# Three input transfers at the head of an encoder layer: the norm's row to GpSimd's queue, a token tile from ScalarE's queue to SyncE's

## The chip, the cores and the metric

The kernel runs on one core of one Trainium2 chip. A core has TensorE (matrix products), VectorE and ScalarE (elementwise work), GpSimd (called POOL in the profile) and SyncE (SP), which only issues transfers. SP, ScalarE and POOL each have a queue of their own for transfers; the core's 16 DMA engines carry out what the three queues hand them. The metric is the device time of one execution in microseconds (us), and the smaller is the better.

## The reference

One layer of an encoder over 1024 tokens of 1024 float32 values:

```python
h = swiglu(rmsnorm(x, ffn1_pre_g), w_gate, w_up, w_down)
x = x + 0.5 * rmsnorm(h, ffn1_post_g)
...                                  # neighbourhood and dilated attention
x = x + 0.5 * rmsnorm(swiglu(rmsnorm(x, ffn2_pre_g), ...), ffn2_post_g)

def rmsnorm(x, g):
    y = xf * lax.rsqrt(jnp.mean(xf * xf, axis=-1, keepdims=True) + NORM_EPS)
    return y * g
def swiglu(x, w_gate, w_up, w_down):
    return (jax.nn.silu(x @ w_gate) * (x @ w_up)) @ w_down
```

The change touches only the start of the first line: the norm of the first 512 tokens with the gain row `ffn1_pre_g`, and the first products with `w_gate`.

## The kernel before

A matrix product is done in three TensorE passes over operands that are split into a high and a low part of a rounded format (`hi`, `lo`: ScalarE rounds with a copy, VectorE subtracts). The products of a 2x2 block scheme follow one another for the whole program; the profile's lines L466, L467 and L472 are the three passes of the first feed-forward product, L783 the second.

Nothing of that can start before the first 512 tokens are normed and transposed. This is the head of the program, and it is written out by hand, in the order in which each engine is to run it (`ordered` keeps that order on TensorE, VectorE and ScalarE):

- `x0` is the input; `xs[0]` to `xs[3]` are tiles of 128 tokens. Tiles 0 and 1 are loaded in two halves of 512 columns each, tiles 2 and 3 whole. In the trace all are `x<-in_x_dram`: L1637 for the halves, L1648 for tile 2, L1649 for tile 3.
- The gain row (4 KB, one partition) goes to the first row of `xn[0]` (L1639, `xn<-in_ffn_pre_g_dram`). `spread_gain` has TensorE multiply it by a row of ones, so that PSUM holds it in all 128 partitions (L344, `gps`), in two halves of two passes each. ScalarE copies each half to `gain` (L345).
- `square` forms sums of squares: ScalarE for tile 0 and for the first half of tile 1 (L166), VectorE for the second half (L1665). `rstd_by_sqrt` makes 1/sqrt of them: two small steps on VectorE (L330, L331), a square root on ScalarE (L332), four more on VectorE.
- `scaled` multiplies the tokens by that and by the gain (L1672, VectorE), `op0.one` transposes them on TensorE (L174) and splits them (L181, L182).
- `graw` are the raw weights of the first blocks, in halves: L1647 the first halves of blocks 0 and 1, L1651 the second halves, L1652 block 2. `parts` splits them (`hi0`, `lo0`, ..., L1683 and L1686).

On ScalarE the order is: square of tile 0, square of tile 1's first half, first gain copy, square root, `hi0`, second gain copy, square of tile 2, the two splits of the transposed tiles, `hi1`, square of tile 3's half.

Each transfer signals one of eight semaphores, which the framework gives out in turn, apart for the hardware queues (SP and ScalarE) and for POOL's; the ninth transfer waits for the one that had its semaphore before.

Of the kernel before, what the change touches and what calls it, by code (L numbers as in the profile page):

```python
# [336 lines left out]
def spread_gain(c, t, row, one):  # L337

    nc = c.nc
    copies = []  # L340
    for h in range(2):
        sl = slice(h * T, h * T + T)
        ps = c.psm.tile([P, T], F32, tag="mm", name="gps")
        nc.tensor.matmul(ps, one, row[:, sl], start=True, stop=True)  # L344
        copies.append(lambda sl=sl, ps=ps: nc.scalar.copy(t[:, sl], ps))  # L345
    return t, *copies
# [1052 lines left out]
def layer(tc, a, out):  # L1399
    nc = tc.nc  # L1400
    c = Ctx(tc)
    with ExitStack() as ctx:
# [26 lines left out]
        x0 = [a["x"][t * P:(t + 1) * P, :] for t in range(8)]  # L1429
# [51 lines left out]
        def gate_pairs(which, op, wg, wu, early):  # L1481
            return PairGemm(c, op, [(wg[f], wu[f]) for f in range(NF)], early, GatePairs(c, which))

        def ffn(which, op, prep, pg, get, turns, sums, more, post, pre, src, dst, begin=None, tables=()):
# [7 lines left out]
            if begin:  # L1492
                left_pool(e)
            begun = begin(pg) if begin else ()
            plan(pg.early, turns)
            r = sub()
# [119 lines left out]
        with ExitStack() as order:  # L1616
# [9 lines left out]
            half = [slice(0, T), slice(T, D)]  # L1626
            first_junk = [c.xp.tile([P, D], F32, tag="s", name="junk", bufs=2)]
            w2 = c.xp.tile([P, D], F32, tag="x1", name="w2", bufs=2)
            xn = [c.xp.tile([P, D], F32, tag="xn", name="xn", bufs=c.xn) for _ in range(2)]
            gain = c.xp.tile([P, D], F32, tag="pre", name="gain", bufs=1)  # L1630
            xs = {t: c.xp.tile([P, D], F32, tag="x", name="x", bufs=4) for t in range(4)}
# [3 lines left out]
            for t in range(2):  # L1635
                for h, q in enumerate((nc.sync, nc.scalar)):
                    q.dma_start(xs[t][:, half[h]], x0[t][:, half[h]])  # L1637
                    if (t, h) == (0, 0):
                        nc.sync.dma_start(xn[0][:1], a["ffn1_pre_g"])  # L1639
            op0.gain, *gains = spread_gain(c, gain, xn[0][:1], xn[1][:1, :P])  # L1640

            def begin(pg):
                for b in range(2):
                    pg.raw[b] = c.wg.tile([P, 2, T], F32, tag="g", name="graw")
                pg.raw[2] = w2.rearrange("p (i x) -> p i x", i=2)
                for b in range(2):
                    nc.sync.dma_start(pg.raw[b][:, 0], pg.srcs[b][0][:, half[0]])  # L1647
                nc.scalar.dma_start(xs[2], x0[2])  # L1648
                nc.sync.dma_start(xs[3], x0[3])  # L1649
                for b in range(2):  # L1650
                    nc.sync.dma_start(pg.raw[b][:, 1], pg.srcs[b][0][:, half[1]])  # L1651
# [89 lines left out]
                while keeps:  # L1741
# [8 lines left out]
                                    {0: [F(4, 5), L(6, 7)], 2: [F(6, 7)], 3: [U(4)], 5: [U(5)], 6: [U(6)], 7: [U(7)]},  # L1750
                                    down_sums(a["wd1"], ts1), value_sums(a["wv"], tsv),
                                    a["ffn1_post_g"], a["mix_pre_g"], x0, x1, begin,
                                    bias_steps(c, *[a[k] for k in ("na_rel_bias", "t5_rel_bias", "onehot", "lncount", "cmask")]))

# [17 lines left out]
            pg = PairGemm(c, op, [(a["wqk"][p], a["wqk"][8 + p]) for p in QK_ORDER], 8, QKPairs(c))  # L1772
# [163 lines left out]
        with ordered():  # L1936
# [18 lines left out]
            pg = gate_pairs(3, op, a["wg2"], a["wu2"], 11)  # L1955
# [94 lines left out]
```

## Time and profile before

| | |
|---|---|
| time, median of 3 runs | 1828.1 us (1826.97 to 1828.38) |
| profiled execution, its own time | 1828.32 us |
| its span, first to last instruction | 1826.5 us |
| TensorE busy in the span | 1808.7 us, 99% |
| VectorE, ScalarE, POOL busy | 1309.8, 832.1, 352.3 us |

The span is 1.8 us shorter than the profiled execution's time, which is 0.2 us above the median of the runs. All times inside the program are counted from the start of the span. In a row of the timeline the first number is the start, the second how long the instruction (or the run of like instructions, with their count behind x) took; the bracket is how long the engine had been idle, and what ended it. "SPq" and "ACTq" are the issuing of transfers, not the transfers themselves.

### The profile page before, as it was taken

The page shows a single profiled execution, that of the slowest core. Times are in us where ns is not written, and L with a number is a line of the kernel's source. Part 1 is how long each engine was busy: PE and PEld are TensorE (multiplying, and loading weights), DVE is VectorE, ACT ScalarE, POOL GpSimd, SP SyncE. Part 2 cuts the span into 40 slices and gives each one's busy share as a digit, 9 for nine tenths or more (in the row PEclk, how much of TensorE's full clock was granted, in tenths as well). Part 3 has the DMA queues.
Part 4 walks back from the last instruction along what each step waited for, and adds up shares of the span by engine and source line. Part 5 has one row for each costly group of instructions (what it writes and reads, how often), then busy time and mean ns, then how long its engine had stood idle before and what let it go on. Part 6 is the DMA issues. An engine that isn't in the chain of part 4 may idle for free.

```text
span 1826.5 us, 25169 instructions
## 1 busy us (share of the span) xinstructions
PE 1808.7 (99%) x8876; PEld 1522.9 (83%) x8876; DVE 1309.8 (72%) x2225; ACT 832.1 (46%) x1495; POOL 352.3 (19%) x583
## 2 busy tenths in 40 slices
PE   8999999999999999999999999999999999999998
PEld 6888888888888888888999998888888888888886
DVE  6878877776466878477666856778877777664557
ACT  6622233334443656234688765654223333354433
POOL 2223321112021123232344100221111111110000
PEclk9999999999999999999999999999999999999999
DMA  7756566557888858868687523594655566596564
GB/s 277 263 182 215 166 226 224 203 208 260 306 302 307 288 200 265 265 226 294 198 264 254 184 97 116 192 309 162 196 179 196 201 221 223 185 349 196 193 230 143
DMA packets 172769, 409.28 MB, mean 224 GB/s; under 512 B 20401, under 2 KB 42321, under 8 KB 170594
## 3 DMA queue, kind: packets, MB, share of 16 engines
q1 hardware_dynamic: 124450, 246.07, 40.9%
q0 software_dynamic: 47184, 159.51, 24.0%
q10 hardware_dynamic: 1008, 2.10, 0.3%
q8 instruction: 70, 1.15, 0.3%
q14 instruction: 57, 0.47, 0.1%
HBM read 280.09 MB, written 132.56 MB: 226 GB/s over the span
## 4 chain that ended last, share of the span: by engine, by line
PE 92%; DVE 3%; DMA 2%; ACT 1%; issue 1%; SPq 0%; DVEq 0%; ACTq 0%
PE accp L783 26%; PE mmp L467 17%; PE mmp L466 17%; PE mmp L472 17%; PE po L1215 2%; PE ptp L1095 2%; PE po L1331 2%; PE accp L357 1%; PE accp L359 1%; PE accp L358 1%; PE sp L1182 1%; PE trp L174 1%; PE sp L1315 1%; DMA praw<-in_wd_dram 1%; DMA graw<-in_wg_dram 1%
## 5 line engine op out<-in xcount | busy, mean ns | idle before, releaser
L466 PE MATMUL mmp<-x,whi 128*128 128x512 f32 (+1 forms) x1464 | 571.8, 391 | 1.7 <-ACT x L181 1.4
L467 PE MATMUL mmp<-x,whi 128*128 128x512 f32 (+1 forms) x1464 | 569.2, 389 | 0.8 <-DVE x L182 0.7
L783 PE MATMUL accp<-pw 128*128 128x512 f32 x1800 | 411.2, 390 | 0.4 <-ACT hb L804 0.4
L783 PEld LDWEIGHTS accp<-pw 128*128 128x128 f32 x1800 | 337.2, 188 | 70.5 <-ACT hb L804 0.8
L472 PE MATMUL mmp<-x,wlo 128*128 128x512 f32 (+1 forms) x1464 | 390.6, 389 | 0.0
L466 PEld LDWEIGHTS mmp<-x,whi 128*128 128x128 f32 x1464 | 275.7, 188 | 59.6 <-ACT x L181 2.2
L467 PEld LDWEIGHTS mmp<-x,whi 128*128 128x128 f32 x1464 | 275.7, 188 | 57.4 <-DVE x L182 1.6
L472 PEld LDWEIGHTS mmp<-x,wlo 128*128 128x128 f32 x1464 | 274.7, 188 | 56.8
L751 DVE TENSOR_TENSOR pw<-praw,pw 128x1024 fp32r<-128x1024 f32 (+1 forms) x181 | 201.2, 1150 | 126.0 <-ACT pw L750 125.1
L750 ACT CAST pw<-praw 128x1024 fp32r<-128x1024 f32 (+1 forms) x181 | 168.8, 983 | 207.4 <-PE accp L783 162.6
L456 ACT CAST whi<-wraw 128x1024 fp32r<-128x1024 f32 x126 | 132.7, 1053 | 187.5 <-PE mmp L467 161.9
L457 DVE TENSOR_TENSOR wlo<-wraw,whi 128x1024 fp32r<-128x1024 f32 x126 | 153.3, 1218 | 2.5 <-ACT whi L456 2.5
L693 POOL DMA_DIRECT2D g<-sg x44 | 24.0, 545 | 428.5 <-DVE sg L686 243.0
L481 ACT COPY s<-mmp 128x512 f32<-128x512 f32 x52 | 30.6, 589 | 131.3 <-PE mmp L472 121.5
L456 ACT CAST whi<-traw 128x512 fp32r<-128x512 f32 x52 | 32.3, 621 | 122.9 <-DVE traw L554 100.0
L645 DVE TENSOR_TENSOR c<-mmp,u 128x512 f32<-128x512 f32 x52 | 35.9, 691 | 69.9 <-PE mmp L472 69.8
L553 DVE TENSOR_TENSOR wraw<-wraw 128x1024 f32<-128x1024 f32 x52 | 63.6, 1224 | 18.1 <-DMA wraw<-in_wu_dram 17.2
L783 PE MATMUL accp<-pw,x 128*128 128x512 f32 x312 | 71.8, 390 | 0.0
L1085 DVE CUSTOM_DVE_ANT_0 s<-sp,g 128x256 f32<-128x256 f32 (+1 forms) x128 | 48.3, 413 | 30.2 <-PE sp L1182 24.5
L783 PEld LDWEIGHTS accp<-pw,x 128*128 128x128 f32 x312 | 58.3, 188 | 12.4 <-DVE pw L751 0.3
L632 DVE TENSOR_TENSOR c<-mmp,v 128x512 f32<-128x512 f32 x52 | 35.8, 689 | 34.1 <-PE mmp L472 34.0
L1331 PE MATMUL po<-vs,pt 128*128 128x128 f32 x352 | 49.9, 276 | 0.0
(280 smaller groups left out, 2489.8 us busy)
## 6 DMA issues: line engine op xcount, KB each, us to landing
praw<-g SPq DMA_DIRECT2D x70, 512.0 KB
wraw<-in_wg_dram SPq DMA_DIRECT2D x44, 512.0 KB
wraw<-in_wu_dram SPq DMA_DIRECT2D x44, 512.0 KB
tr<-in_wd_dram SPq DMA_DIRECT2D x44, 512.0 KB
g<-sg POOLq DMA_DIRECT2D x88, 256.0 KB, 5.4
ts<-tr POOLq DMA_DIRECT2D x22, 1024.0 KB, 4.7
praw<-ts SPq DMA_DIRECT2D x88, 256.0 KB
praw<-in_wd_dram SPq DMA_DIRECT2D x66, 256.0 KB
```

Source lines behind the costliest of these rows:

```text
L456: nc.scalar.copy(hi, raw)
L457: nc.vector.tensor_sub(lo, raw, hi.bitcast(F32))
L466: mm(out, hi[:, i, sl], xhi[:, k, cols], start=not go_on and k == 0, stop=False, skip_group_check=go_on)
L467: mm(out, hi[:, i, sl], xlo[:, k, cols], start=False, stop=False, skip_group_check=go_on)
L472: mm(out, lo[:, i, sl], xhi[:, k, cols], start=False, stop=k == 3, skip_group_check=go_on)
L553: nc.vector.tensor_sub(r[:, 0:2], r[:, 1:3], r[:, 0:2])
L750: nc.scalar.copy(hi, raw[:, :m])
L751: nc.vector.tensor_sub(lo, raw[:, :m], hi.bitcast(F32))
L783: c.nc.tensor.matmul(acc[t], a, b, start=not chained and gi == 0 and j == i == 0, stop=end and j + n >= len(ops) and i == len(two) - 1, sk ...
L1085: c.nc.vector.tensor_tensor_reduce(out=s, in0=ps, in1=bias, scale=-1.0, scalar=3e38, op0=ALU.add, op1=ALU.min, accum_out=neg)
L1095: nc.tensor.transpose(ps[:, j, :], src[:, j * P:(j + 1) * P], c.ident)
L1331: nc.tensor.matmul(po[0][:, u], pt[0][:, j, :], vs[:, k0 + j, :], start=j == 0, stop=j == n - 1)
```

## The change

The gain row is issued from POOL's queue and no longer as the second transfer on SP's. Tile 2 is issued from SP's queue, behind the first half of block 0's weights, and no longer as the third transfer on ScalarE's. The halves of tiles 0 and 1 are left alone at the front of SP's and ScalarE's queues.

```diff
             for t in range(2):
                 for h, q in enumerate((nc.sync, nc.scalar)):
                     q.dma_start(xs[t][:, half[h]], x0[t][:, half[h]])
-                    if (t, h) == (0, 0):
-                        nc.sync.dma_start(xn[0][:1], a["ffn1_pre_g"])
+            nc.gpsimd.dma_start(xn[0][:1], a["ffn1_pre_g"])
             op0.gain, *gains = spread_gain(c, gain, xn[0][:1], xn[1][:1, :P])
...
-                for b in range(2):
-                    nc.sync.dma_start(pg.raw[b][:, 0], pg.srcs[b][0][:, half[0]])
-                nc.scalar.dma_start(xs[2], x0[2])
+                nc.sync.dma_start(pg.raw[0][:, 0], pg.srcs[0][0][:, half[0]])
+                nc.sync.dma_start(xs[2], x0[2])
+                nc.sync.dma_start(pg.raw[1][:, 0], pg.srcs[1][0][:, half[0]])
                 nc.sync.dma_start(xs[3], x0[3])
```

SP's queue at the start of the program, before (the gain row is `xn<-in_ffn_pre_g_dram`, the two `x` of 512 columns are the first halves of tiles 0 and 1, the `x` of 1024 columns is tile 3):

```order
L1637 DMA x<-in_x_dram 128x512
L1639 DMA xn<-in_ffn_pre_g_dram 1x1024
L1637 DMA x<-in_x_dram 128x512
L1647 DMA graw<-in_wg_dram 128x512 x2
L1649 DMA x<-in_x_dram 128x1024
L1651 DMA graw<-in_wg_dram 128x512 x2
L1652 DMA w_153<-in_wg_dram 128x1024
```

and with the change:

```order
L1637 DMA x<-in_x_dram 128x512 x2
L1645 DMA graw<-in_wg_dram 128x512
L1646 DMA x<-in_x_dram 128x1024
L1647 DMA graw<-in_wg_dram 128x512
L1648 DMA x<-in_x_dram 128x1024
L1650 DMA graw<-in_wg_dram 128x512 x2
L1651 DMA w_153<-in_wg_dram 128x1024
```

The half of tile 1 now follows the half of tile 0 at once, and tile 2 (L1646) stands between the first halves of the two weight blocks, ahead of tile 3 (L1648).

POOL at the same place, before (`ident` is the unit matrix for the transposes, `ss` the sums of squares, `xn_0` the first store of the normed tokens, much later):

```order
masks.py:197 MEMSET ident 128x128
L1634 MEMSET xn 1x128
masks.py:199 ISA
masks.py:199 AFFINE_SELECT ident<-ident 128x128
L1691 MEMSET ss_219 128x4
L1691 MEMSET ss_220 128x4
L262 DMA xn_0_165<-raw 128x512
```

and with the change:

```order
masks.py:197 MEMSET ident 128x128
L1634 MEMSET xn 1x128
masks.py:199 ISA
masks.py:199 AFFINE_SELECT ident<-ident 128x128
L1638 DMA xn<-in_ffn_pre_g_dram 1x16x64
L1690 MEMSET ss_219 128x4
L1690 MEMSET ss_220 128x4
L262 DMA xn_0_165<-raw 128x512
```

The row's transfer stands behind the making of `ident` and ahead of the two fills of `ss`. On ScalarE the only row that goes is the issue of tile 2; the order of the work on TensorE, VectorE and ScalarE is the same in both kernels to the end of the program.

## The prediction

> **What bounds the kernel now.** I read the page's busy shares first, then TensorE's waits from 30 us to the end, then the chain of work over the first 13 us, and last the DMA queues and the timeline there.
>
> From the page, the busy shares and the chain's shares by engine:
>
> ```profile
> PE 1808.7 (99%) x8876; PEld 1522.9 (83%) x8876; DVE 1309.8 (72%) x2225; ACT 832.1 (46%) x1495; POOL 352.3 (19%) x583
> PE 92%; DVE 3%; DMA 2%; ACT 1%; issue 1%; SPq 0%; DVEq 0%; ACTq 0%
> ```
>
> TensorE's waits after 30 us (first and last of six), and a table of its busy time by stretch (length, busy time and instructions, clock, DMA share, GB/s):
>
> ```profile
> PE trp L174 <- DVE og L1380: 0.4, 1, 0.4
> ...
> PE mmp L466 <- ACT s L481: 0.2, 1, 0.2
> 0.00:12.00 12.00, 5.77 (x13) 1.00 0.83 304
> 30.00:1826.50 1796.50, 1786.49 (x8773) 1.00 0.66 224
> ```
>
> After 30 us TensorE waits six times, 0.4 us at most. So nothing there swallows a shift of the head and nothing there can be won by it: the program's end moves by what TensorE's first product moves. The change can only act in the first 12 us, where TensorE is busy for 5.77.
>
> The chain of work over that stretch (start, length, what):
>
> ```profile
> 0.75 0.39 SPq L1637
> 1.20 0.30 SPq L1639
> 1.56 4.57 DMA x<-in_x_dram
> 6.15 0.72 ACT junk L166 x2
> ...
> 12.65 0.58 PE mmp L467
> ```
>
> The chain is the very thing that the change edits: SP's queue issues tile 0's half, the gain row, and only at 1.56 tile 1's half, which ScalarE waits for until 6.15. Then square, gain copy, square root, norm, transposes, products.
>
> DMA share and rate by stretch (POOL's busy time stands before the clock; share and GB/s are the last two columns), and the packets by queue from 3.5 to 4.25 us (q10 is ScalarE's, q1 is SP's):
>
> ```profile
> 3.50:4.25 0.75, 0.00 (x0) 1.00 0.78 229
> 4.25:5.50 1.25, 0.00 (x0) 1.00 0.99 380
> q10 hardware_dynamic: 95, 0.17, 75.6%
> q1 hardware_dynamic: 9, 0.00, 1.9%
> 9.00:12.00 3.00, 0.00 (x0) 1.00 1.02 403
> ```
>
> From 3.50 to 4.25 SP's queue moved 9 packets and no payload to speak of, while ScalarE's went on with tile 1's second half; the rate fell to 229 GB/s. That is the hole behind the gain row, ahead of the half that the chain waits for.
>
> **The change, part by part.** The rows of the engines concerned (POOL, ScalarE, VectorE, TensorE):
>
> ```profile
> 1.13 0.28 POOL masks.py:199 TENSOR_SCALAR_AFFINE_SELECT ident<-ident 128x128 f32<-128x128 f32 x1
> 3.45 0.20 ACT L1692 ACTIVATE junk<-ss 128x1 f32<-128x1 f32 x1
> 4.23 1.06 ACT L166 ACTIVATE junk<-x 128x1024 f32<-128x1024 f32 x1 [0.57 <-DMA x<-in_x_dram]
> 6.15 0.63 ACT L166 ACTIVATE junk<-x 128x512 f32<-128x512 f32 x1 [0.77 <-DMA x<-in_x_dram]
> 6.78 0.57 ACT L345 COPY gain<-gps 128x512 f32<-128x512 f32 x1
> 7.30 0.20 ACT L332 ACTIVATE e<-v 128x2 f32<-128x2 f32 x1
> 9.07 1.06 ACT L166 ACTIVATE junk<-x 128x1024 f32<-128x1024 f32 x1
> 5.59 0.69 DVE L1665 CUSTOM_DVE_ANT_0 xn<-x 128x512 f32<-128x512 f32 x1 [5.59 <-DMA x<-in_x_dram]
> 6.91 0.16 DVE L330 TENSOR_TENSOR v<-ss 128x2 f32<-128x2 f32 x1 [0.61 <-ACT junk L166]
> 4.40 2.04 PE L344 MATMUL gps<-xn 1*128 1x512 f32 x2 [4.40 <-DMA xn<-in_ffn_pre_g_dram]
> ```
>
> *Tile 1's half, earlier.* It is issued when the row was, at 1.20 and not at 1.56: 0.36 us at least, if issue is all that counts. If it also fills the hole of 0.75 us on SP's queue, 0.75. Tile 1's other half, which had a free queue, reached VectorE at 5.59, so 5.40 is plausible; I take 0.75, since the hole is measured, and 6.15 becomes 5.40. ScalarE could take it then: its square of tile 0 ends at 5.29. The square would be done at 5.40 + 0.63 = 6.03.
>
> *The gain row on POOL.* This is the unknown price. It is issued behind `ident`, at 1.41 (1.13 + 0.28). What POOL's queue takes from issue to landing: first its first transfer (a store, at 16.2 us), then its eight table loads from 111 us on (L965), then its four loads of token tiles from 20.8 us on (L1624):
>
> ```profile
> L262 POOL DMA_DIRECT2D xn<-raw x1: 703/703/703, 16.2 to 16.2; - x1
> DMA to landing us min/median/max: 2.5/2.5/2.5
> DMA to landing us min/median/max: 2.3/3.1/3.7
> DMA to landing us min/median/max: 5.4/7.3/9.6
> ```
>
> The row is 4 KB in an empty POOL queue, beside the loads of tiles 0 and 1. Nearest are the table loads (small reads of memory) and the store (first of its queue). I take 3.0, close to the table loads' median: it lands at 4.4, when TensorE started on it before. The low end, 2.3, gives 3.7; the far ends, 5.4 and 9.6 of the token loads, which are large and stood behind POOL's own stores, give 6.8 and 11.0. POOL's two fills of `ss` slip behind the issue, by the 0.70 that the first issue took: done at about 2.3, wanted at 3.45 by ScalarE. That is 1.1 us of cover, and past it ScalarE waits for tile 0 until 4.23 anyhow: nothing.
>
> *The first gain copy.* It needs the first two TensorE passes, which end at 4.40 + 2.04 = 6.44, and ScalarE, now free at 6.03. Before, ScalarE was last (6.78); now the gain row is what is late next. The copy goes from 6.78 to about 6.47: **0.3 us earlier, not 0.75**. The square root, 0.52 behind the copy, goes from 7.30 to 7.0. It also needs VectorE's two steps, which took from 6.91 to 7.30 before; the two halves' sums are there at 6.2 and 6.3, so the root could start at 6.7 or 6.8. That doesn't bind; it is the limit if the row comes early, at 0.5 us in all.
>
> *Tile 2 on SP's queue.* It loses its early place on ScalarE's queue. Ahead of it now stand tiles 0 and 1 and a quarter of a megabyte of weights; with it that is 1.8 MB from 2.0 us, at 380 GB/s done at 6.8, and at the 229 GB/s of a lone queue from 5.0 on done at 8.4. ScalarE wants it at 9.07 before, at about 8.7 now. Behind it on SP's queue are the first half of block 1's weights and tile 3, which ScalarE takes up later:
>
> ```profile
> 11.77 0.62 ACT L1683 CAST whi<-graw 128x512 fp32r<-128x512 f32 x1
> 12.29 0.63 ACT L166 ACTIVATE junk<-x 128x512 f32<-128x512 f32 x1
> 8.07 0.62 ACT L1683 CAST whi<-graw 128x512 fp32r<-128x512 f32 x1 [0.56 <-DMA graw<-in_wg_dram]
> 10.43 0.59 ACT L181 CAST x<-trp 128x512 fp32r<-128x512 f32 x1 [0.21 <-PE trp L174]
> SPq L1649 <- DMA x<-in_x_dram: 1.3, 1, 1.3
> ```
>
> At 403 GB/s, which SP's queue alone reached from 9 to 12 us, they are there at 7.6 and 8.9, three us ahead of their use. Block 0's half (the wait of 0.56 at 8.07) only gains, as tile 2 no longer shares the engines with it. SP's own wait of 1.3 us ahead of tile 3, for a semaphore, goes as well, since one transfer fewer is ahead of it. Cost: nothing; if that cover fails, ScalarE's square of tile 2 has 0.34 us to spare before the transposed tile (10.43 less 0.3 is 10.1; the square ends at 9.8).
>
> *ScalarE without an issue.* Its table load starts 0.45 earlier and then waits for tile 0 as before: nothing.
>
> *Sum.* The square root 0.3 earlier, and all behind it in the head. The rest of the head is unchanged work in unchanged order, and the shift is kept to the end. 1828.1 - 0.3 = **1827.8 us** (the profiled execution's 1828.32 would be 1828.0; I forecast from the median). A measurement of this kernel can tell about 0.2%, 3.7 us; the whole wait that is edited is 0.77. So the verdict is "same" unless a rival with a price of several us holds.
>
> A rule speaks against the change. The Trainium skill, DMA: Bandwidth & Descriptors, section "Issuing engines are not separate DMA queues", says that transfers from all issuing engines run on the same 16 DMA engines, so that another issuer saves the sequencer's time alone. By it the term would be 0.36 and not 0.75. The sum by it stays at -0.3, as the gain row limits both. The hole of 0.75 us on one queue at 229 GB/s speaks for more than issue time.
>
> **The rivals.**
>
> *The gain row comes late (slower).* The copy turns later than 6.78 once TensorE starts on the row after 4.71, that is, once the row takes over 3.3 us from POOL's issue. The store's 2.5 and the table loads' median of 3.1 lie under that, their longest over it. At 3.7 us the copy would start at 7.2: +0.4, 1828.5. At 5.4 it would start at 8.9: +2.1, 1830.2. At 9.6 it would be +6.3, 1834.4; to be slower by 0.2% the row must take 7.0. Against the far ends: the token loads stood behind other transfers on POOL's queue, the row stands behind none. For them: the engines are as busy here (0.78 to 0.99) as a queue can find them.
>
> *TensorE's step to full speed moves by a stretch.* Its first products run at half pace (the start of each, 256 columns):
>
> ```profile
> 13.03 0.41 PE L466 MATMUL mmp<-x,whi 128*128 128x256 f32 x1
> 13.24 0.41 PE L467 MATMUL mmp<-x,whi 128*128 128x256 f32 x1
> 17.73 0.28 PE L467 MATMUL mmp<-x,whi 128*128 128x256 f32 x1
> 17.85 0.28 PE L466 MATMUL mmp<-x,whi 128*128 128x256 f32 x1
> ```
>
> 0.21 from start to start until about 17, 0.12 after. It is a step some 4.5 us behind the first dense product at 12.65, though the clock column says 1.00 throughout. If an earlier start meets that step 4.5 us sooner or later, 4.5 x (1 - 0.12/0.21) = 1.9 us go either way: 1826.2 or 1829.7. The three runs before lie 1.4 us apart, which such a step would explain, so it may fall differently in any run. The Trainium skill, TensorE: Matmul & The Clock Gate, Part 1, has the gate open on a free-running window of 3413 ns that doesn't reset at a kernel's start; as an estimate from that page the step would be worth 1.5 us.
>
> *Nothing moves.* Tile 1's half may be held by memory rather than by its place, and the row land 0.3 later: 1828.1. For it: the DMA share is 0.78 even inside the hole, so there is less free than the rate suggests.
>
> *Tile 2 is late.* At 229 GB/s for the whole stretch from 2.0 us it would land at 10.0, its square end at 11.1, one us behind the transposed tile: +1.0, 1828.8. Against it: 380 and 403 GB/s with the engines fed.
>
> **How the numbers follow.** The forecast (0.1 to 0.5 us faster): 0.50. Row late by under 5.4 us in all: 0.17; over 7.0 us: 0.03. The step: 0.08 each way. Nothing: 0.10. Tile 2: 0.04. Only the very late row leaves the band of 0.2%, with 0.01 on the other side for what I don't see: faster 0.01, same 0.96, slower 0.03. The range runs from the step sooner (1826.2) to the row at 5.4 us (1830.2), which leaves the far row and sums of two rivals outside; the forecast's own is 1827.3 to 1828.1.
>
> **What would show it.** Tile 1's square on ScalarE at 5.3 to 5.8 in place of 6.15, with ScalarE's wait for it gone; TensorE starting on the gain row at 4.1 to 4.7; the gain copy at 6.4 to 6.7 and released by TensorE; tile 2's square with no wait for a transfer ahead of it; the first dense product at 12.3 to 12.5 in place of 12.65; TensorE's waits after 30 us still under half a us each. I am wrong if TensorE starts on the row after 4.71, if ScalarE waits for tile 2, or if a wait of over 1 us appears on TensorE later than 30 us.

## The result and the profile after

| | before | after |
|---|---|---|
| time, median of 16 runs each | 1828.3 us (1826.87 to 1830.46) | 1831.06 us (1829.99 to 1834.5) |
| ratio, with its 95% interval | | 1.0016 (1.0009 to 1.0023) |
| TensorE starts on the gain row, three profiles | 4.40, 4.40, 4.24 | 6.92, 7.04, 7.15 |
| first gain copy on ScalarE, three profiles | 6.78, 6.47, 7.85 | 8.99, 9.11, 9.23 |

The change costs 2.8 us by the medians; the interval of the ratio makes that 1.6 to 4.2 us (0.0009 and 0.0023 of 1828.3). It is under the 0.2% that the prediction called "same", but on the other side of zero from its 0.3 us gain, and 0.9 us above the top of its range. The first profile of the changed kernel is of an execution of 1834.5 us, the slowest of the 16, so two more were taken of each kernel. In the head, the rows of the changed kernel up to the first L467 product lie within 0.3 us of each other in all three.

The timeline of the changed kernel's head (start, length, engine, line, operation; in the bracket how long the engine had been idle, and for what):

```profile
1.52 0.67 POOL L1638 DMA_DIRECT2D xn<-in_ffn_pre_g_dram  x1
2.18 0.17 POOL L1690 MEMSET ss<- 128x4 f32 x2
4.26 1.06 ACT L166 ACTIVATE junk<-x 128x1024 f32<-128x1024 f32 x1 [1.09 <-DMA x<-in_x_dram]
5.36 0.63 ACT L166 ACTIVATE junk<-x 128x512 f32<-128x512 f32 x1
6.92 3.75 PE L344 MATMUL gps<-xn 1*128 1x512 f32 x4 [6.92 <-DMA xn<-in_ffn_pre_g_dram]
8.99 0.59 ACT L345 COPY gain<-gps 128x512 f32<-128x512 f32 x1 [2.91 <-PE gps L344]
9.48 0.21 ACT L332 ACTIVATE e<-v 128x2 f32<-128x2 f32 x1
11.18 1.06 ACT L166 ACTIVATE junk<-x 128x1024 f32<-128x1024 f32 x1
14.82 0.58 PE L467 MATMUL mmp<-x,whi 128*128 128x256 f32 x1
```

Tile 1's half is squared at 5.36 with no wait (the row has no bracket), as was meant. But ScalarE then stands idle for 2.91 us, because TensorE got the gain row only at 6.92. The square root (L332) follows the copy, and the first L467 product comes at 14.82 where it came at 12.65: 2.2 us later.

The chain of work of the same profile over the head (start, length, what): the transfer of a 4 KB row is now its longest piece, in the place where tile 1's half stood.

```profile
1.52 5.26 DMA xn<-in_ffn_pre_g_dram
6.78 0.14 issue
6.92 2.06 PE gps L344 x2
8.97 0.02 issue
8.99 0.59 ACT gain L345
...
14.82 0.58 PE mmp L467
```

TensorE's two longest waits after 30 us in that profile (total, times, longest):

```profile
PE accp L783 <- ACT hb L804: 2.2, 1, 2.2
PE po L1331 <- DVE pt L1097: 2.0, 1, 2.0
```

They lie at 476 and 1021 us, far from the change. That they belong to the run and not to the change is not settled: the changed kernel's other two profiles have no wait on `hb` over 0.2 us, and this wait on `po` (L1331) is 1.2 us in one and none in the other; the kernel before has 0.35 us on `hb` in one of its three, and on the same `po` none, 1.0 and 0.3 us.

So how much does the head lose? TensorE's 200th product, at about 51 us, gives a fixed point behind it. Counted from the first profile of before, its start lies 0.00, -0.10 and +0.59 us away in the three profiles of before, and +1.51, +1.51 and +2.59 in those of after: means of 0.16 and 1.87, a loss of **1.7 us** in the head, and the two groups don't overlap. The 2000th product, at about 456 us, has each of these shifts within 0.02 us, so up to there nothing is added or lost. Behind it they change in steps, the largest at about 472, 987, 1012 and 1243 us (in the time of the first profile of before), by other amounts in each profile of the same kernel: the last product lies 0.00, -0.24 and -0.55 us away in before, and +6.19, +2.58 and +0.23 in after. So the three profiles don't tell where the other 1.1 of the measured 2.8 us come from.

### The profile page after: what moved, and what is told of

Its sections match the earlier page's. It is cut to its first block, busy times and chain, and to the rows that moved or that the text cites. A ratio compares the mean times of both kernels' runs of the same rounds, so it can differ in the third digit from the quotient of the medians.

```text
span 1832.7 us, 25171 instructions
## 1 busy us (share of the span) xinstructions
PE 1809.5 (99%) x8876; PEld 1523.8 (83%) x8876; DVE 1308.5 (71%) x2225; ACT 831.5 (45%) x1495; POOL 352.4 (19%) x584
## 4 chain that ended last, share of the span: by engine, by line
PE 81%; issue 10%; DMA 3%; DVE 3%; POOL 1%; ACT 1%; POOLq 0%; DVEq 0%; SPq 0%; ACTq 0%
PE accp L783 26%; PE mmp L467 14%; PE mmp L472 14%; PE mmp L466 14%; PE po L1215 2%; PE ptp L1095 2%; PE po L1331 2%; PE sp L1182 1%; PE trp L174 1%; DMA rg<-ob 1%; PE sp L1315 1%; PE accp L358 1%; PE accp L357 1%; PE accp L359 1%; POOL g L717 1%
## 5 line engine op out<-in xcount | busy, mean ns | idle before, releaser
L467 PE MATMUL mmp<-x,whi 128*128 128x512 f32 (+1 forms) x1464 | 568.8, 389 | 0.7 <-DVE x L182 0.6
L467 PEld LDWEIGHTS mmp<-x,whi 128*128 128x128 f32 x1464 | 275.6, 188 | 57.4 <-DVE x L182 1.5
L1331 PE MATMUL po<-vs,pt 128*128 128x128 f32 x352 | 49.9, 276 | 2.0 <-DVE pt L1097 2.0
```

What stands on the lines that cost most here:

```text
L467: mm(out, hi[:, i, sl], xlo[:, k, cols], start=False, stop=False, skip_group_check=go_on)
L1331: nc.tensor.matmul(po[0][:, u], pt[0][:, j, :], vs[:, k0 + j, :], start=j == 0, stop=j == n - 1)
```

## The experiments

All edits are against the changed kernel. Two theories stood against each other on the cause: that the row's transfer has a fixed price on POOL's queue whenever it is POOL's first, and that it is slow because of the loads that run beside it. The second has two forms: any full stream of loads does it, or it takes both hardware queues (SP's and ScalarE's) together. A third thing to part was the row from tile 2, the change's other half.

### Tile 2's move alone

```diff
             for t in range(2):
                 for h, q in enumerate((nc.sync, nc.scalar)):
                     q.dma_start(xs[t][:, half[h]], x0[t][:, half[h]])
-            nc.gpsimd.dma_start(xn[0][:1], a["ffn1_pre_g"])
+                    if (t, h) == (0, 0):
+                        nc.sync.dma_start(xn[0][:1], a["ffn1_pre_g"])
```

> The gain row back as the second transfer on SP's queue, tile 2 on SP's queue as in the change. Theory (the row's place on POOL's queue makes the whole loss): TensorE starts on the row at 4.4 us as before, the first gain copy at 6.5 to 6.8, the time within 0.5 us of before. Rival (tile 2's new place costs part of it): ScalarE waits for tile 2 or tile 1's half, the time at least 1 us over before.

Measured: 1829.51 us (median of 11; the kernel before 1828.42, of 27), ratio 1.0005 (0.9997 to 1.0014). Its timeline:

```profile
4.08 3.75 PE L344 MATMUL gps<-xn 1*128 1x512 f32 x4 [4.08 <-DMA xn<-in_ffn_pre_g_dram]
6.63 0.56 ACT L345 COPY gain<-gps 128x512 f32<-128x512 f32 x1
9.22 1.06 ACT L166 ACTIVATE junk<-x 128x1024 f32<-128x1024 f32 x1 [0.33 <-DMA x<-in_x_dram]
```

With the row back on SP's queue the gain copy is where it was before, so the row is what costs. Tile 2 on SP's queue comes just too late here: ScalarE waits 0.33 us for it. At 51 us the shift is +0.32. By the medians the run is 1.1 us over the kernel before: the 0.5 us of the theory is missed, and the rival, which had ScalarE wait for tile 2 and at least 1 us, is met. But the interval runs from 0.5 us less to 2.6 us more, so the time settles nothing; there is no sign of a gain that would have justified the move.

### The row's move alone

```diff
-                nc.sync.dma_start(pg.raw[0][:, 0], pg.srcs[0][0][:, half[0]])
-                nc.sync.dma_start(xs[2], x0[2])
-                nc.sync.dma_start(pg.raw[1][:, 0], pg.srcs[1][0][:, half[0]])
+                for b in range(2):
+                    nc.sync.dma_start(pg.raw[b][:, 0], pg.srcs[b][0][:, half[0]])
+                nc.scalar.dma_start(xs[2], x0[2])
```

> The gain row on POOL's queue, tile 2 third on ScalarE's queue as before. Theory, in two forms. Traffic: the row's packets wait until the loads of tiles 0 and 1 are through, TensorE starts on it at about 6.9 us, the time 1.5 to 2.8 us over before. Two queues: POOL's queue gets nothing while both hardware queues have work, so the row also waits for tile 2 on ScalarE's queue; TensorE starts on it at 8 us or later and the time is over 3 us above before. Rival, fixed price: POOL's first transfer takes 5.3 us from issue whatever else runs; 6.9 us as well.

Measured: 1832.52 us (median of 11), ratio 1.0016 (1.0007 to 1.0025): about the whole loss. At 51 us the shift is +2.33. Its timeline:

```profile
7.71 3.75 PE L344 MATMUL gps<-xn 1*128 1x512 f32 x4 [7.71 <-DMA xn<-in_ffn_pre_g_dram]
9.79 0.58 ACT L345 COPY gain<-gps 128x512 f32<-128x512 f32 x1 [3.49 <-PE gps L344]
```

The row now lands 6.06 us after its issue, later than in the changed kernel, though nothing on POOL differs. What differs is ScalarE's queue, which has tile 2 behind tile 1's half and so stays busy. The start of 7.71 lies between the numbers expected (6.9, and 8 or later). The packets say what tile 2 added. No packet of POOL's queue, q0, runs before 5.4 us here, and none before 5.2 in the changed kernel: the first one is as late in both. But here the row's 32 packets take from 5.4 to 7.2 us, and there from 5.3 to 6.4. POOL's queue from 5.4 to 7.3 us (packets, MB, share):

```profile
q0 software_dynamic: 32, 0.00, 1.4%
```

### Nothing else moving while the row travels

The row is issued first of all loads, and fills on POOL of the first buffers to be loaded hold the loads back until it has landed.

```diff
+            nc.gpsimd.dma_start(xn[0][:1], a["ffn1_pre_g"])
+            for t in range(2):
+                for h in range(2):
+                    nc.gpsimd.memset(xs[t][:, half[h]], 0.0)
+            for t in (2, 3):
+                nc.gpsimd.memset(xs[t][:, :1], 0.0)
+            nc.gpsimd.memset(w2[:, :1], 0.0)
...
-            nc.gpsimd.dma_start(xn[0][:1], a["ffn1_pre_g"])
...
+                for b in range(2):
+                    for i in range(2):
+                        nc.gpsimd.memset(pg.raw[b][:, i, :1], 0.0)
```

> The whole change, but the loads of tiles 0 to 3 and of the first weights are held back behind fills by POOL, so that the row, issued at 1.5 us, has the DMA engines to itself for 2 us and more. Its time says nothing, as every load is late. Traffic and two queues: the row lands 2.3 to 3.0 us after its issue, TensorE starts on it at 4.0 to 4.6. Fixed price: 5.3 us after issue, TensorE at 6.9.

Measured. The row's own group (its issue, ns and start; then the time from issue to landing):

```profile
L1635 POOL DMA_DIRECT2D xn<-in_ffn_pre_g_dram x1: 667/667/667, 1.5 to 1.5; - x1
DMA to landing us min/median/max: 1.8/1.8/1.8
```

The table by stretch while the row travels (stretch, its length, busy time of the five engines, TensorE's clock, DMA share, GB/s):

```profile
1.50:3.40 1.90, 0.00 (x0) 0.00 (x0) 0.00 (x0) 0.00 (x0) 1.88 (x4) 1.00 0.01 2
```

The same transfer, issued at the same 1.52 on the same queue, lands after 1.83 us (5.26 in the changed kernel) when the DMA engines are idle, share 0.01, and TensorE starts on it at 3.48. The theory of a fixed price for POOL's first transfer falls. Of the 5.26 us, 3.4 are due to the loads beside it. Even so, q0 has no packet from 1.5 to 2.85 us; all 32 run from 2.85 to 3.1:

```profile
q0 software_dynamic: 32, 0.00, 9.6%
```

So some 1.35 us pass from the issue to the first packet with nothing in the way. In the changed kernel these are 3.75 us (1.52 to 5.27): 2.4 of the 3.4 us lie ahead of the first packet, and the rest behind it. The time of this version, 1833.5 us in one run, says nothing here, since the loads start late.

The Trainium skill, DMA: Bandwidth & Descriptors, section "Anatomy of one DMA — SWDGE (gpsimd) path", gives a fixed cost of about 2.0 us for a transfer issued from GpSimd. The quiet run's 1.83 agrees, and the loaded head doesn't. The same page, section "Queues, rings and completion order", has each DMA engine take turns between its queues packet by packet. A packet there is a run of rows, where the profile counts each row. As an estimate from that rule, with 8 rows of 2 KB on each engine as a packet of a half tile, two queues and the 335 GB/s that the changed kernel moved from 1.8 to 5.1 us over 16 engines, the row would wait 32 KB at 21 GB/s, 1.6 us at most; the runs show 2.4 ahead of its first packet and 3.4 in all.

### The row on POOL, all four halves on SP's queue

```diff
             for t in range(2):
-                for h, q in enumerate((nc.sync, nc.scalar)):
-                    q.dma_start(xs[t][:, half[h]], x0[t][:, half[h]])
+                for h in range(2):
+                    nc.sync.dma_start(xs[t][:, half[h]], x0[t][:, half[h]])
```

> The whole change, but all four halves of tiles 0 and 1 go through SP's queue, so that ScalarE's queue is empty and one hardware queue alone has work while the row waits. Theory A, two hardware queues together keep POOL's packets out: with one, the row lands within 3.7 us of its issue at 1.52, TensorE starts on it by 5.3 us while the tiles are still loading. Theory B, any full stream of loads issued ahead of it keeps the row back until those loads are through: TensorE starts at 6.5 us or later, as the tiles take at least as long through one queue. The tiles themselves come later, so its time says little.

Measured, in the timeline:

```profile
5.79 3.75 PE L344 MATMUL gps<-xn 1*128 1x512 f32 x4 [5.79 <-DMA xn<-in_ffn_pre_g_dram]
6.19 0.63 ACT L166 ACTIVATE junk<-x 128x512 f32<-128x512 f32 x1 [0.50 <-DMA x<-in_x_dram]
7.87 0.59 ACT L345 COPY gain<-gps 128x512 f32<-128x512 f32 x1 [0.96 <-PE gps L344]
```

4.14 us from issue to landing: between what the two forms gave (3.7 at most, or TensorE at 6.5 and later). The bytes of the tiles are the same, so one busy hardware queue delays the row less than two do, and far more than none. The row's packets ran from 3.6 us on here, while the tiles were still loading. In the changed kernel POOL's queue, q0, moved nothing at all until tiles 0 and 1 were nearly in; the DMA queues of that kernel from 2.0 to 5.2 us, and then from 5.2 to 6.3 (packets, MB, share; other queues' packets there are loads of tiles and weights):

```profile
q1 hardware_dynamic: 324, 0.60, 56.8%
q10 hardware_dynamic: 288, 0.52, 44.5%
```

```profile
q1 hardware_dynamic: 114, 0.26, 99.2%
q0 software_dynamic: 31, 0.00, 2.4%
```

In the first stretch q0 has no line: not one of its packets ran in 3.2 us, beside 612 of the two hardware queues. By the quiet run, they could have run from 2.9 us on. With one hardware queue the first came 2.06 us after the issue (1.52 to 3.58), with two 3.75, with none 1.35.

### The row first in the program's order, on POOL

```diff
-        make_identity(nc, c.ident)
...
+            nc.gpsimd.dma_start(xn[0][:1], a["ffn1_pre_g"])
             ...
+            make_identity(nc, c.ident)
...
-            nc.gpsimd.dma_start(xn[0][:1], a["ffn1_pre_g"])
```

> The whole change, with the row as the very first work of POOL, ahead of the fill of the unit matrix: issued at about 0.75 us in place of 1.52. Traffic: its packets are there before the tile loads fill the engines, TensorE starts on it at 4.5 us or sooner, the gain copy at 6.0 to 6.6, the time 0 to 0.5 us under before. Fixed price of 5.3 us: TensorE starts at 6.1, the copy at 8.2, the time about 1.4 us over before. Two queues: as the change, 6.9, unless its packets come ahead of the tiles'.

Measured: 1830.01 us (median of 11), ratio 1.0005 (0.9996 to 1.0013). Its timeline:

```profile
1.29 0.67 POOL L1633 DMA_DIRECT2D xn<-in_ffn_pre_g_dram  x1 [0.84 <-POOLq L2039]
5.92 3.75 PE L344 MATMUL gps<-xn 1*128 1x512 f32 x4 [5.92 <-DMA xn<-in_ffn_pre_g_dram]
8.00 0.58 ACT L345 COPY gain<-gps 128x512 f32<-128x512 f32 x1 [1.81 <-PE gps L344]
```

The expectations missed: TensorE starts at 5.92, not at 4.5 or sooner, and the fixed price (6.1), which the quiet run rules out, lies nearest. Two more things. The issue comes at 1.29 and not at the 0.75 at which the other queues issue first: POOL had been idle 0.84 us, and only four fills of constants, done by 0.45, are ahead of it. And an issue 0.23 us earlier brings the landing 1.0 us forward (5.79 for 6.78), 4.49 us after the issue. The row still meets the loads, and still makes ScalarE wait. At 51 us the shift is +0.83: over half of the head's loss is back, and the interval of the time holds no change.

### The row on ScalarE's queue, first and third

First, ahead of the halves:

```diff
+            nc.scalar.dma_start(xn[0][:1], a["ffn1_pre_g"])
             for t in range(2):
                 for h, q in enumerate((nc.sync, nc.scalar)):
                     q.dma_start(xs[t][:, half[h]], x0[t][:, half[h]])
-            nc.gpsimd.dma_start(xn[0][:1], a["ffn1_pre_g"])
```

> The change's places for tiles 1 and 2, but the gain row is the first transfer on ScalarE's queue, and nothing of it is on POOL's. If the loss lies in POOL's queue under load: the row lands by 3.8 us, tile 0's second half is 0.45 us later than in the change at most, the gain copy starts at 6.2 to 6.6 (6.78 before), the time 0 to 0.5 us under before. Rival, the row makes a hole of 0.75 us wherever it stands on a hardware queue: tile 0 is late by that, the copy at 6.8 or later, the time as before or over.

Measured: 1830.61 us (median of 11), ratio 1.0014 (1.0005 to 1.0023). Its timeline:

```profile
2.30 1.19 PE L344 MATMUL gps<-xn 1*128 1x512 f32 x1 [2.30 <-DMA xn<-in_ffn_pre_g_dram]
6.43 1.06 ACT L166 ACTIVATE junk<-x 128x1024 f32<-128x1024 f32 x1 [2.76 <-DMA x<-in_x_dram]
8.10 0.56 ACT L345 COPY gain<-gps 128x512 f32<-128x512 f32 x1
```

The row is there at 2.30, and the loss is about that of the change (+2.37 at 51 us): now tile 0's second half, behind the row on that queue, is late, and ScalarE begins its first square at 6.43 and not at 4.26. That half is issued 0.56 us later (1.31 for 0.75), which is the smaller part of it; the rival had given 0.75. From 1.5 to 3.0 us ScalarE's queue (q10) moved 2 packets:

```profile
q10 hardware_dynamic: 2, 0.00, 0.9%
```

in the changed kernel, 66 in the same stretch. Here the row of one partition ahead of a tile on a hardware queue held that tile back by more than its issue. It looks like the hole that the prediction saw behind the row on SP's queue, and here it is longer: ScalarE's queue has no packet from 1.9 to 3.1 us.

Third, behind the halves of tiles 0 and 1:

```diff
-            nc.gpsimd.dma_start(xn[0][:1], a["ffn1_pre_g"])
+            nc.scalar.dma_start(xn[0][:1], a["ffn1_pre_g"])
```

> The change with the gain row third on ScalarE's queue, behind the halves of tiles 0 and 1, in place of POOL's; it is issued at about 1.7 us, as late as on POOL's. If being behind the tiles' megabyte is what makes the row late: TensorE starts on it at 5.5 to 7.0 us, like the change. If it is POOL's queue that yields to the others: TensorE starts at 5.0 us or sooner, as a hardware queue's row took 3.2 us from issue before.

Measured, in the timeline:

```profile
5.48 3.75 PE L344 MATMUL gps<-xn 1*128 1x512 f32 x4 [5.48 <-DMA xn<-in_ffn_pre_g_dram]
7.55 0.59 ACT L345 COPY gain<-gps 128x512 f32<-128x512 f32 x1 [1.25 <-PE gps L344]
```

The shift at 51 us is +0.95; the time is 1827.85 us in one run beside one of the kernel before at 1831.65, which orders nothing. The start of 5.48 meets neither number expected (5.5 to 7.0, or 5.0 and sooner). The row lands 1.4 us sooner than on POOL, though issued 0.16 later, and 1.1 later than in the kernel before. So of the 2.5 us by which TensorE's start moved, a little less than half comes from standing behind the tiles instead of between them (0.48 us of it from the later issue, 1.68 for 1.20), and the rest from POOL's queue. These are one profile each.

On POOL's queue the row also travels in another form, as 32 packets of at most 256 bytes, where on a hardware queue its 4 KB go in one. Whether that form costs time of its own was not run.

No version among these is shown to beat the kernel before.

### Both kernels again

The changed kernel unchanged, for a second and a third profile, and the kernel before likewise:

> The change once more, for a second profile of it. If the waits of 2.2 us on TensorE at 476 us and of 2.0 us at 1021 us belong to the change, they stand here again at that length; if they are a matter of the single run, they are shorter, and the shift that the head makes (1.5 us at 50 us) is what is left.

> The change a third time, for its head and for its waits after 30 us. Head: TensorE starts on the row at 6.8 to 7.1 us again. Later waits of over 0.5 us on TensorE stand at other places or lengths than in the two earlier profiles if they are a matter of the run; the same place and length each time if they belong to the change.

> The kernel before once more, for a second profile. If the waits at 476 us and about 1016 us come and go by themselves, they differ here from the 0.4 us and nothing of its first profile; if they belong to the change, they are the same as there within 0.2 us.

> The kernel before a third time. Tile 1's half is taken up by ScalarE anywhere from 5.4 to 6.2 us if its place behind the row is only a part of what decides; at 6.1 us again if the hole of the first profile is the rule. TensorE starts on the row at 4.4.

Measured, in single runs: after 1830.79 and 1828.54 us, before 1828.02 and 1827.7 us. The row of the changed kernel took 5.38 and 5.50 us to land; 5.26 was no outlier. Tile 1's half in the kernel before, in the second and the third profile:

```profile
5.77 0.63 ACT L166 ACTIVATE junk<-x 128x512 f32<-128x512 f32 x1
```

```profile
7.22 0.63 ACT L166 ACTIVATE junk<-x 128x512 f32<-128x512 f32 x1 [1.77 <-DMA x<-in_x_dram]
```

5.77 with no wait, 6.15 in the profile that the prediction had, and 7.22: the wait that the change was to remove is 0 to 1.77 us, by the run. In the changed kernel the same square starts at 5.36, 5.43 and 5.37, never after a wait.

## Why the prediction was wrong

- **Tile 1's half, earlier.** The start came out: 5.40 was forecast and 5.36, 5.43, 5.37 measured. But these squares follow tile 0's square without a wait, so they show only that the half had landed by then. The base of 6.15 was one sample of 5.77 to 7.22, so the gain of 0.75 is only as good as that sample. By the 0.36 us of issue alone, which the prediction took from the Trainium skill, DMA: Bandwidth & Descriptors, section "Issuing engines are not separate DMA queues", the half would have come at 5.79 from 6.15, which doesn't fit, and at 5.41 or sooner from 5.77, which does; the runs don't decide it.
- **The gain row on POOL.** This is the step that failed: 3.0 us from issue to landing were taken, 5.26, 5.38 and 5.50 measured. The prediction picked the nearest rows by size and by the queue's emptiness, the table loads and POOL's first store. It left out how full the DMA engines were. From the kernel before, the stretches of the store, of the table loads and of the token loads that it set aside (the DMA share and GB/s are the last two columns):

```profile
16.00:19.00 3.00, 2.88 (x19) 2.47 (x17) 1.38 (x3) 1.78 (x4) 1.26 (x2) 1.00 0.45 171
111.00:117.00 6.00, 6.00 (x28) 4.98 (x27) 4.54 (x7) 1.77 (x3) 2.90 (x6) 1.00 0.49 139
20.00:31.00 11.00, 10.09 (x61) 8.46 (x60) 6.92 (x11) 8.21 (x16) 6.63 (x13) 1.00 0.83 300
```

The rows that gave 2.5 and 3.1 us were taken at shares of 0.45 and 0.49. The head runs at 0.78 to 0.99, as the prediction quoted itself, and the rows taken at a like share, 0.83, gave 5.4 us as their least. With that number the prediction's own sum stood under the first rival: TensorE late, copy at 8.9, +2.1, 1830.2. The copy came at 8.99. The mechanism was among the rivals, and got a chance of 0.17, which ended at 5.4; the 5.38 and 5.50 measured had no chance of their own.

That 5.4 fits so well is luck in part. The token loads are of 512 KB each, the row is 4 KB, and beside them it was POOL's queue itself that had most of the traffic (queues from 20 to 31 us: packets, MB, share):

```profile
q0 software_dynamic: 704, 2.43, 63.2%
q1 hardware_dynamic: 223, 0.85, 19.0%
```

Nor does the share set the price alone: with one hardware queue the row took 4.14 us, and its packets got in from 3.6 us on at a share of 0.98 (3.6 to 5.8 us). In the kernel before ScalarE's queue moves nothing between 8 and 1809 us, and POOL's first transfer is issued at 16.2: none of the rows that the prediction looked at had POOL's queue beside two busy hardware queues, so they held no price for this.

- **The issue on POOL** is at 1.52 and not at 1.41: 0.11 us between `ident` and the issue were left out. Small.
- **POOL's fills of `ss`** behind the issue: right, at 2.18, and nobody waited.
- **The first gain copy.** The logic held (TensorE and not ScalarE's square is what is late next), with the wrong sign, since TensorE started 2.2 us past the deciding point of 4.71.
- **Tile 2 on SP's queue.** Right in the changed kernel, where its square at 11.18 waits for no transfer; but only because the row gave it two more microseconds. With the row on time it is wanted at 8.9, waits 0.33 and starts at 9.22. So "nothing" is short by that. The rival's 1.0 us was not seen in the head (+0.32 at 51 us).
- **The shift is kept to the end.** Only in part. It is kept from the 200th product to the 2000th, at 456 us, and not ahead of these or behind them: the third profile of the changed kernel is 2.59 us late at 456 us and 0.23 at its last product. That nothing behind 30 us swallows a shift was read from one profile. In the head of the first profile some of it came back: the first L467 product is 2.2 us later, the 200th product 1.5. TensorE's products in the changed kernel (start, length):

```profile
15.20 0.42 PE L466 MATMUL mmp<-x,whi 128*128 128x256 f32 x1
15.41 0.42 PE L467 MATMUL mmp<-x,whi 128*128 128x256 f32 x1
17.53 0.28 PE L467 MATMUL mmp<-x,whi 128*128 128x256 f32 x1
17.64 0.28 PE L466 MATMUL mmp<-x,whi 128*128 128x256 f32 x1
```

The step from 0.21 to 0.12 us between starts is reached at 17.5 here, 2.7 us behind the first L467 product. In the kernel before it falls among the transposes, whose starts go from 0.21 to 0.11 us apart at 17.07, 4.4 us behind that product. So the step didn't move with the product, and the later start cost less than it should have. The other two profiles of before have it at 17.6 and 17.0 (5.3 and 3.3 us behind the product), the second of the changed kernel at 17.7 (2.7). The third has it only at 20.3 (5.3 behind), and there nothing came back: +2.59. The Trainium skill, TensorE: Matmul & The Clock Gate, Part 1, has the gate open on a window that runs free of the kernel; that the distance from the first product runs from 2.7 to 5.3 us agrees with it. Behind the head, the later waits named above differ from run to run by 1 to 2 us each. The shift of 1.7 us at 51 us lies inside the interval of 1.6 to 4.2 for the whole; whether the last 1.1 us have a cause of their own stays open.
- **The range** ended at the row's 5.4 us (1830.2) with nothing for the spread of the later waits. The first profile shows both at once, the late row and 2.2 and 2.0 us of later waits.

Open is also what keeps POOL's packets out while two hardware queues are busy. The runs show that they stay out (no packet of q0 from 2.0 to 5.2 us, where the quiet run has the first at 2.87) and how the landing depends on the queues (1.83 us with none busy, 4.14 with one, 5.26 to 5.50 with two, 6.06 with tile 2 added on the second). They don't show what holds the first packet.

## What to carry to other kernels

Price a moved transfer by a row taken beside the same traffic on the other queues, not by one of the same size or on the same queue; where the trace has none, a wide range is honest. Here rows taken at half the load gave 2.5 and 3.1 us, and the row took 5.26 to 5.50. Moving a small transfer aside to free the bulk's queue made it wait for the bulk; in this kernel none of the four other places tried for the row is shown to do better than the one it had, between the halves on SP's queue. And before a wait of 0.77 us is booked as a gain, see it in more than one profile: this one was 0, 0.77 and 1.77.

## What the runs showed of the hardware

- A 4 KB load on POOL's queue lands after 1.83 us with idle DMA engines, of which 1.35 pass ahead of its first packet, and after 6.06 with both hardware queues kept busy. That POOL's queue gets no packet in for 3.75 us after the issue, and not merely its share, I had not expected.
- A row of one partition is a poor neighbour on a hardware queue too: ahead of a tile on ScalarE's queue it cost the tile's square 2.2 us (6.43 for 4.26, of which 0.56 are the later issue), with 2 packets on that queue from 1.5 to 3.0 us where 66 had run.
- POOL's first transfer issues at 1.29 (one profile) with nothing ahead of it since 0.45, while SP and ScalarE issue theirs at 0.75.
